# Gated linear attention on one core: the decay of the chunk states applied to the queries, and the steps of two heads interleaved on TensorE

## The chip, the cores and the metric

The kernel runs on one core of a Trainium2 chip. The metric is the device time of one execution in microseconds (us). The engines are named as in the profile: PE (TensorE, with PEld for its weight loads), DVE (VectorE), ACT (ScalarE), POOL (GpSimd), and SP, which issues the DMAs.

## The reference, cut to what matters

The program is one encoder layer on two sequences of 512 tokens: a SwiGLU half step, a mixer of gated linear attention (GLA, 4 heads) beside grouped-query attention, an output projection, a second SwiGLU half step and a gated embedding. The change lies in GLA, in one direction of which the reference computes, by chunks of 64 tokens (`b` is the running sum of the log decay within a chunk):

```
cum = cumsum(log_a)          # within a chunk
mid, last = cum at the chunk's middle, at its end
scores  = (q * exp(cum - mid)) @ (k * exp(mid - cum)).T, masked
o_intra = scores @ v
upd     = (k * exp(last - cum)).T @ v
state_{c+1} = exp(last_c) * state_c + upd_c
o_inter = (q * exp(cum)) @ state_c
o = o_intra + o_inter
```

The forward direction includes the token itself, the backward one doesn't. The sum of both goes through an RMS norm per head and a swish gate.

## The kernel before

The GLA steps are short, and between them TensorE works on the output projection of the other half of the mixer. TensorE's order is written by hand: generators yield after each piece of work, and `main.weave(order(), pieces, end)` puts one piece of GLA after every one or two ticks of `main`, where a tick is three products of 128x512 (L707, called main products below). The other engines' order is made by a scheduler from the order in which the code issues work and from its dependences. Matmul results that aren't main products go to a pool of four PSUM banks (`pd`); a step that needs a bank waits until the earlier user's readers are done.

Two generators `A` and `B` do the two sequences, each with four heads h, in pairs that share `pre`. The steps are:

- `pre(hp)` (L990 to L1008): loads log decay and q, k of two heads, sums the decay with a product (`b`), takes exponentials on ScalarE (`E`), and makes on VectorE the scaled queries and keys `z` (tile `qk1`, named qk in the profile): eight products of 64x512. Rows 0 to 63 hold the forward direction, 64 to 127 the backward one. `R` (128 x 8) holds for each chunk the decay between the middles of neighbouring chunks.
- `one(h)` has three pieces. kT: TensorE transposes the keys (L1022), ScalarE copies them. U: eight products of keys and values give the chunks' updates in two banks (L1029); ScalarE starts the states W with the first and the last chunk (L1036, L1037), and VectorE runs the recurrence over the chunks, six updates in each direction, alternating (L1039, L1041); then GpSimd multiplies all states by R (L1042, L1043). S: eight products give the scores of both directions (L1051), and VectorE copies them under the masks into A (L1053).
- `two_a(h)`: TensorE adds A times v (L1062) and scaled queries times W (L1065) in one bank; ScalarE squares it (osq, L1068), VectorE sums (oss, L1070), makes the norm's factor and multiplies four blocks with the gate into Gh (L1073).
- `two_b(h)`: TensorE transposes Gh (L1080), ScalarE and VectorE write it into mixG (L1081, L1082), which the output projection reads later.

States are kept relative to a chunk's middle, hence the factor R between the recurrence's state and the one that a query of the next chunk uses. The evacuations of the main products on VectorE (L1099, L1101, with statistics at L509) and the splits of weights into two parts (L137 on ScalarE, L138 on GpSimd or VectorE) run beside all this.

In `order()`, a pair of heads runs one(0), one(1), two_a(0), two_a(1), then pre of the next pair, then two_b(0), two_b(1).

Of the kernel before, what the change touches and what calls it, by code (L numbers as in the profile page):

```python
# [13 lines left out]
ALU = mybir.AluOpType  # L14
# [6 lines left out]
NT = 4  # L21
# [9 lines left out]
PLAN = dict(s0=102,  # L31
            s1=112,
            d0=(8, 14, 20, 26, 32),
            sB=(52, 56, 60, 75, 77),
            d1=(90, 96, 102, 108, 117),
            A=(157, 159, 160),
            seg=((2, 132), (2, 142), (18, 160), (18, 170), (43, 193), (43, 216), (178, 334)),
            b=(4, 3),
            end=415)
# [675 lines left out]
class Middle:  # L715
# [246 lines left out]
    def gla(self, s):  # L962
        nc, L = self.nc, self.L
        f, bw = slice(0, 64), slice(64, 128)
        T = {}

        def pre(hp):
            if hp == 0:
                T["mx"] = L.xp.tile([128, 4, 2, 512], F32R, tag="x", name="mixG")
                self.mix[s, 0] = T["mx"]  # L970
                T["A"] = self.vp.tile([128, 2, NT, 128], F32, tag="v", name="A")
                nc.gpsimd.memset(T["A"], 0.0)
            lq = self.m8("lq", (128, 2, 2, 512))
            l, qk = lq[:, 0].rearrange("p d (t c) -> p d t c", t=NT), lq[:, 1]
            for t in range(NT):
                nc.sync.dma_start(l[:, :, t], self.spill["l", s][t].rearrange("p (d c) -> p d c", d=2)[:, :, hp * 128:(hp + 1) * 128])
            for i in range(2):
                nc.sync.dma_start(qk[:, i], self.spill["gqk", s][2 * i + hp])
            yield
            R = [self.sp.tile([128, 8], F32, tag=f"R{e}", name=f"R{e}", bufs=2) for e in range(2)]  # L980
            E = self.m8("E", (128, 2, 2, 512))
            z = self.m8("qk1", (128, 2, 2, 512))
            for e in range(2):
                T["z", 2 * hp + e], T["R", 2 * hp + e] = z[:, e], R[e]
            for dr in range(2):
                sc = self.sp.tile([128, 2, 8], F32, tag="sc", name="sc")
                for hf in range(2):
                    b = L.bank_d().rearrange("p (a n) -> p a n", a=2)
                    for a in range(2):
                        nc.tensor.matmul(b[:, a, :132], l[:, dr, 2 * hf + a], self.L.U[:, dr], start=True, stop=True)  # L990
                    for j, sg in ((0, 1.0), (1, -1.0)):
                        L.expln(E[:, dr, j, hf * 256:(hf + 1) * 256].rearrange("p (a n) -> p a n", a=2),
                                             b[:, :, :128], AF.Exp, scale=sg)
                    nc.vector.tensor_copy(
                        sc[:, :, hf * 4:hf * 4 + 4].rearrange("p k (a c) -> p a k c", a=2),
                        b[:, :, 128:132].rearrange("p a (k c) -> p a k c", k=2))
                    if hf == 0:
                        yield
                ex = self.sp.tile([128, 7], F32, tag="ex", name="ex")
                if dr == 0:  # L1000
                    nc.vector.tensor_tensor(ex, sc[:, 1, 0:7], sc[:, 0, 1:8], ALU.add)
                else:
                    nc.vector.tensor_tensor(ex, sc[:, 1, 1:8], sc[:, 0, 0:7], ALU.add)
                for e in range(2):
                    rs, rd = slice(64 * e, 64 * e + 64), slice(64 * dr, 64 * dr + 64)
                    L.expln(R[e][rd, 1 - dr:8 - dr], ex[rs], AF.Exp)
                    for i in range(2):
                        nc.vector.tensor_tensor(z[rd, e, i], qk[rs, i], E[rs, dr, i], ALU.mult)  # L1008
                yield

        def one(h):
# [6 lines left out]
            q1, k1 = T["z", h][:, 0], T["z", h][:, 1]  # L1018
            R = T["R", h]
            b = L.bank_d()  # L1020
# [2 lines left out]
            kT = self.m2("kT", shape=(128, NT, 128))  # L1023
            nc.scalar.activation(kT.rearrange("p a n -> p (a n)"), b, AF.Copy)
            yield
            U = [L.bank_d().rearrange("p (c n) -> p c n", c=4) for _ in range(2)]
            for c in range(8):
                rw = slice(64 * (c % 2), 64 * (c % 2) + 64)
# [9 lines left out]
            for c in range(1, 7):  # L1038
                nc.vector.scalar_tensor_tensor(W[f, c + 1], W[f, c], R[f, c:c + 1], up(c, f), ALU.mult, ALU.add)  # L1039
                cb = 7 - c  # L1040
                nc.vector.scalar_tensor_tensor(W[bw, cb - 1], W[bw, cb], R[bw, cb:cb + 1], up(cb, bw), ALU.mult, ALU.add)  # L1041
            nc.gpsimd.tensor_tensor(W[f, 1:8], W[f, 1:8], R[f, 1:8].unsqueeze(2).to_broadcast([64, 7, 128]), ALU.mult)  # L1042
            nc.gpsimd.tensor_tensor(W[bw, 0:7], W[bw, 0:7], R[bw, 0:7].unsqueeze(2).to_broadcast([64, 7, 128]), ALU.mult)  # L1043
            yield
            A = T["A"][:, h % 2]
            S = [L.bank_d().rearrange("p (a n) -> p a n", a=NT) for _ in range(2)]
            for t in range(NT):
                ts = slice(t * 128, (t + 1) * 128)
                for dr in range(2):
                    rd = slice(64 * dr, 64 * dr + 64)  # L1050
                    nc.tensor.matmul(S[dr][:, t], k1[rd, ts], q1[rd, ts], start=True, stop=True)  # L1051
            for dr in range(2):
                nc.vector.copy_predicated(A, self.L.mask[:, dr].unsqueeze(1).to_broadcast([128, NT, 128]), S[dr])  # L1053
            T["h", h] = gv, G, W, A
            yield

# [87 lines left out]
def build(tc, d, outs):  # L1144
    nc = tc.nc
    ctx = ExitStack()
    with ctx:
# [36 lines left out]
        with ExitStack() as mctx:  # L1184
# [50 lines left out]
            def order():  # L1235
                yield from A00
                for _ in range(PLAN["b"][0]):
                    yield
                yield from A[1](0)
                yield from A[1](1)  # L1240
                yield from A[2](0)
                yield from A[2](1)
                yield from A[0](1)
                yield from A[3](0)
                yield from A[3](1)
                yield from A[1](2)
                yield from A[1](3)
                yield from A[2](2)
                yield from A[2](3)
                yield from B[0](0)  # L1250
                yield from A[3](2)
                yield from A[3](3)
                yield from B[1](0)
                yield from B[1](1)
                yield from B[2](0)
                yield from B[2](1)
                yield from B[0](1)
                yield from B[3](0)
                yield from B[3](1)
                yield from B[1](2)  # L1260
                yield from B[1](3)
                yield from B[2](2)
                yield from B[2](3)
                for _ in range(PLAN["b"][1]):
                    yield
                yield from B[3](2)
                yield from B[3](3)
            main.weave(order(), 60 - len(PLAN["A"]) + PLAN["b"][0] + PLAN["b"][1], PLAN["end"])
            main.end()

# [158 lines left out]
```

## Time and profile before

| | us |
|---|---|
| three runs | 1990.23, 1979.57, 1983.87 |
| median | 1983.87 |
| profiled execution, its time | 1983.58 |
| its span | 1981.8 |
| GLA's stage, first kT to last two_b (1031.68 to 1165.77 in the span) | 134.09 |
| busy in that stage: PE / DVE / ACT / POOL | 115.78 / 107.47 / 42.58 / 54.83 |

The times are of the whole program; the span is from the first to the last instruction of the profiled execution. Times in timelines count from the span's start. A row of a timeline has start, duration, engine, line, operation, tile written and read, and, in brackets, how long the engine was idle before it and what ended that. A row of the windows has the stretch, its length, and per engine busy time and instructions, then the mean granted clock of TensorE and the DMA's share and rate. A row of the waits names who waited for whom: total, times, longest. In rows of TensorE on these small tiles the profile counts a product of full precision twice (x16 for eight).

### The profile page before, as it was taken

The numbers are of one execution on the slowest core, as the hardware profiler recorded it, in microseconds if no ns is written. First come the engines' busy times: TensorE is split into PE (matmuls) and PEld (weight loads), VectorE is DVE, ScalarE is ACT, GpSimd is POOL, SyncE is SP. The second block draws the span as 40 slices with busy tenths as digits, with TensorE's granted clock in tenths as the row PEclk, the third lists the DMA queues.
The fourth block names the chain that finished last, engine by engine and source line by source line (L and its number), as shares of the span: only waits on it lengthen the run. The fifth ranks groups of instructions, "written<-read, shape, count | busy, mean of one in ns | idle before, by whom it ended". The sixth has DMA issues, their size and how long they took to land. (4 is left out here: it accounts for less than half of the span.)

```text
span 1981.8 us, 25356 instructions
## 1 busy us (share of the span) xinstructions
PE 1879.1 (95%) x8838; PEld 1534.9 (77%) x8838; DVE 1367.1 (69%) x2068; ACT 883.4 (45%) x1670; POOL 950.2 (48%) x710
## 2 busy tenths in 40 slices
PE   7999999999999797989998888999999999799999
PEld 5788888888788686877876667888888888588787
DVE  7856566574656974778778879566566575855973
ACT  5445444444221444757852337445444444221342
POOL 0665565554761254342234343654665555762253
PEclk9999999999999998999999999999999999899999
DMA  4425444478666233222443331435434478576142
GB/s 177 156 105 177 168 150 152 148 288 337 268 248 211 73 126 111 77 80 91 133 143 101 94 117 66 158 109 185 161 141 170 155 297 338 206 267 255 54 128 85
DMA packets 104959, 322.22 MB, mean 163 GB/s; under 512 B 11008, under 2 KB 38400, under 8 KB 99456
## 3 DMA queue, kind: packets, MB, share of 16 engines
q1 hardware_dynamic: 104832, 320.61, 44.9%
q8 instruction: 70, 1.15, 0.2%
q14 instruction: 57, 0.47, 0.1%
HBM read 218.85 MB, written 101.71 MB: 162 GB/s over the span
## 5 line engine op out<-in xcount | busy, mean ns | idle before, releaser
L138 POOL TENSOR_TENSOR w<-raw,w 128x512 fp32r<-128x512 f32 (+1 forms) x372 | 511.4, 1385 | 773.8 <-ACT w L137 714.7
L137 ACT ACTIVATE w<-raw 128x512 fp32r<-128x512 f32 (+1 forms) x586 | 363.5, 624 | 444.5 <-POOL raw L269 107.8
L425 PE MATMUL pm<-X,w 128*128 128x512 f32 x1848 | 435.0, 393 | 11.0 <-ACT X L137 8.2
L269 POOL TENSOR_TENSOR raw<-raw 128x512 f32<-128x512 f32 x240 | 348.0, 1458 | 155.6 <-DMA raw<-in_wgu 81.7
L425 PEld LDWEIGHTS pm<-X,w 128*128 128x128 f32 x1848 | 347.9, 189 | 89.5 <-ACT X L137 8.8
L425 PE MATMUL pd<-X,w 128*128 128x512 f32 x1320 | 309.2, 392 | 2.9 <-DVE w L138 2.2
L138 DVE TENSOR_TENSOR w<-raw,w 128x512 fp32r<-128x512 f32 x214 | 220.3, 1035 | 126.0 <-ACT w L137 116.4
L425 PEld LDWEIGHTS pd<-X,w 128*128 128x128 f32 x1320 | 248.5, 189 | 58.0 <-DVE w L138 3.0
L536 PE MATMUL pm<-w,XB 128*128 128x512 f32 x864 | 202.5, 394 | 5.5 <-POOL w L138 5.4
L707 PE MATMUL pm<-w,h1T 128*128 128x512 f32 (+1 forms) x768 | 183.9, 382 | 22.6 <-ACT gr L749 11.4
L536 PEld LDWEIGHTS pm<-w,XB 128*128 128x128 f32 x864 | 163.3, 190 | 42.8 <-POOL w L138 9.1
L138 DVE TENSOR_TENSOR hs<-sg,hs 128x512 fp32r<-128x512 f32 (+1 forms) x182 | 143.8, 810 | 49.5 <-ACT hs L137 48.4
L137 ACT ACTIVATE hs<-sg 128x512 fp32r<-128x512 f32 (+1 forms) x182 | 98.4, 561 | 164.8 <-DVE sg L391 64.4
L707 PEld LDWEIGHTS pm<-w,h1T 128*128 128x128 f32 x768 | 135.9, 194 | 45.0 <-ACT gr L749 11.7
L536 PE MATMUL pd<-w,XB 128*128 128x512 f32 x648 | 151.2, 393 | 15.5 <-issue 14.8
L536 PEld LDWEIGHTS pd<-w,XB 128*128 128x128 f32 x648 | 122.8, 190 | 42.0 <-issue 15.2
L523 DVE TENSOR_TENSOR Y<-Y,pm 128x512 f32<-128x512 f32 x104 | 70.6, 684 | 61.5 <-PE pm L536 61.3
L523 DVE TENSOR_TENSOR Y<-Y,pd 128x512 f32<-128x512 f32 x88 | 59.9, 684 | 60.0 <-PE pd L536 57.3
L707 PE MATMUL pm<-w,h3T 128*128 128x512 f32 x384 | 90.8, 393 | 0.9 <-DVE h3T L662 0.9
L371 DVE TENSOR_TENSOR sg<-u,pm 128x512 f32<-128x512 f32 x22 | 15.1, 687 | 109.3 <-PE pm L425 109.3
L707 PEld LDWEIGHTS pm<-w,h3T 128*128 128x128 f32 x384 | 71.2, 188 | 15.8 <-DVE h3T L662 1.4
L652 ACT ACTIVATE pd<-pd,c_lnT 128x512 f32<-128x512 f32 x48 | 36.0, 752 | 100.4 <-PE pd L650 100.4
(237 smaller groups left out, 2554.0 us busy)
## 6 DMA issues: line engine op xcount, KB each, us to landing
hs<-hs SPq DMA_DIRECT2D x126, 512.0 KB, 2.6
XB<-hs SPq DMA_DIRECT2D x42, 1536.0 KB, 6.8
raw<-in_wgu SPq DMA_DIRECT2D x88, 512.0 KB, 3.5
raw<-in_wd SPq DMA_DIRECT2D x36, 512.0 KB, 6.4
hs_t<-hs SPq DMA_DIRECT2D x56, 256.0 KB, 2.5
XB<-hs_t SPq DMA_DIRECT2D x26, 512.0 KB, 5.2
raw<-in_wout SPq DMA_DIRECT2D x16, 512.0 KB, 3.6
raw<-in_wpg SPq DMA_DIRECT2D x16, 512.0 KB, 3.5
```

The lines of the kernel that those rows point to most:

```text
L137: first = nc.scalar.activation(hi, raw, AF.Copy)
L138: (eng or nc.vector).tensor_tensor(lo, raw, hi.bitcast(F32), ALU.subtract)
L269: (sums or self.nc.gpsimd).tensor_tensor(o(), x(), y(), ALU.subtract)
L371: add = lambda o, x, y: nc.vector.tensor_tensor(o, x, y, ALU.add)
L425: nc.tensor.matmul(bank, w[:, a, kt * 128:(kt + 1) * 128], X[k][:, kt, b], start=(k in (0, 1, 4) and kt == 0 and m == 0), stop=(kt == 3 an ...
L523: nc.vector.tensor_tensor(yv, yv, bank, ALU.add)
L536: nc.tensor.matmul(b[t], h[:, a, t * 128:(t + 1) * 128], d[:, c], start=(k in (0, 4, 1) and g == 0 and x == 0), stop=(g == len(H) - 1 and ...
L652: nc.scalar.activation(p, p, AF.Identity, scale=self.lnT[:, c:c + 1], bias=self.lnT[:, c + 8:c + 9])
L707: nc.tensor.matmul(banks[t][:, :width], x[:, i, t * 128:(t + 1) * 128], w[a][:, j], start=(q == 0 and a == 0 and m == 0), stop=(q == nq - ...
```

## The change

Two things are done. First, the states are no longer multiplied by R on GpSimd. Instead, after the scores have been computed from the scaled queries q1, VectorE multiplies q1 in place by R, chunk by chunk (128x512, R spread over 64 columns), and two_a uses these queries. For that the scores come ahead of the states in `one(h)`, and R is zeroed first (a memset of 128x8 per head on GpSimd), since the chunk without a predecessor now has a factor too. Second, `order()` no longer runs both heads of a pair through one step and then the next: the second head's kT and S come before the first head's two_a, its U comes between the first head's two_a and two_b, and its own two_b comes after the next pair's pre.

```diff
             for e in range(2):
+                nc.gpsimd.memset(R[e], 0.0)
                 T["z", 2 * hp + e], T["R", 2 * hp + e] = z[:, e], R[e]
...
             nc.scalar.activation(kT.rearrange("p a n -> p (a n)"), b, AF.Copy)
             yield
+            A = T["A"][:, h % 2]
+            S = [L.bank_d().rearrange("p (a n) -> p a n", a=NT) for _ in range(2)]
+            for t in range(NT):
+                ts = slice(t * 128, (t + 1) * 128)
+                for dr in range(2):
+                    rd = slice(64 * dr, 64 * dr + 64)
+                    nc.tensor.matmul(S[dr][:, t], k1[rd, ts], q1[rd, ts], start=True, stop=True)
+            for dr in range(2):
+                nc.vector.copy_predicated(A, self.L.mask[:, dr].unsqueeze(1).to_broadcast([128, NT, 128]), S[dr])
+            qc = q1.rearrange("p (c n) -> p c n", c=8)
+            nc.vector.tensor_tensor(qc, qc, R.unsqueeze(2).to_broadcast([128, 8, 64]), ALU.mult)
+            yield
             U = [L.bank_d().rearrange("p (c n) -> p c n", c=4) for _ in range(2)]
...
-            nc.gpsimd.tensor_tensor(W[f, 1:8], W[f, 1:8], R[f, 1:8].unsqueeze(2).to_broadcast([64, 7, 128]), ALU.mult)
-            nc.gpsimd.tensor_tensor(W[bw, 0:7], W[bw, 0:7], R[bw, 0:7].unsqueeze(2).to_broadcast([64, 7, 128]), ALU.mult)
-            yield
...
             T["h", h] = gv, G, W, A
             yield
...
+                def two(H, p, nxt):
+                    g = [H[1](p), H[1](p + 1)]
+                    for j in (0, 0, 0, 1, 1):
+                        next(g[j])
+                        yield
+                    yield from H[2](p)
+                    next(g[1])
+                    yield
+                    yield from H[3](p)
+                    yield from H[2](p + 1)
+                    yield from nxt
+                    for _ in range(PLAN["b"][1] if nxt is last else 0):
+                        yield
+                    yield from H[3](p + 1)
+                last = ()
+                yield from two(A, 0, A[0](1))
+                yield from two(A, 2, B[0](0))
+                yield from two(B, 0, B[0](1))
+                yield from two(B, 2, last)
```

(`H[0]` to `H[3]` are pre, one, two_a and two_b; the removed lines of `order()` called them in the order told above.) Of before and after, what follows is the program's own order on an engine; qk_8660 is the tile of the first pair's queries and keys, gvh the values.

TensorE before, from U of the first head to two_a of the first head:

```order
L1029 MATMUL pd<-gvh,kT 128x128 x8
L707 MATMUL pm<-w,mixA 128x512 x6
L1051 MATMUL pd<-qk_8660 128x128 x8
L707 MATMUL pm<-w,mixA 128x512 x3
L1022 MATMUL pd<-c_ident,qk_8660 128x128 x4
L707 MATMUL pm<-w,mixA 128x512 x3
L1029 MATMUL pd<-gvh,kT 128x128 x8
L707 MATMUL pm<-w,mixA 128x512 x3
L1051 MATMUL pd<-qk_8660 128x128 x8
L707 MATMUL pm<-w,mixA 128x512 x6
L1062 MATMUL pd<-gvh,A 128x128
L1065 MATMUL pd<-W,qk_8660 64x128 x2
```

Here both heads' U and S are done before the first two_a. TensorE after, between the same two steps of the first head:

```order
L1042 MATMUL pd<-gvh,kT 128x128 x8
L707 MATMUL pm<-w,mixA 128x512 x3
L1023 MATMUL pd<-c_ident,qk_8660 128x128 x4
L707 MATMUL pm<-w,mixA 128x512 x3
L1033 MATMUL pd<-qk_8660 128x128 x8
L707 MATMUL pm<-w,mixA 128x512 x3
L1063 MATMUL pd<-gvh,A 128x128
L1066 MATMUL pd<-W,qk_8660 64x128 x2
```

The first head's S now stands ahead of these rows, and the second head's U behind them. TensorE after, from the end of the first head's two_a to the start of the second's:

```order
L707 MATMUL pm<-w,mixA 128x512 x6
L1042 MATMUL pd<-gvh,kT 128x128 x8
L707 MATMUL pm<-w,mixA 128x512 x3
L1081 MATMUL pd<-c_ident,Gh 128x128 x4
L707 MATMUL pm<-w,mixA 128x512 x3
L1063 MATMUL pd<-gvh,A 128x128
L1066 MATMUL pd<-W,qk_8660 64x128 x2
```

Before, only three main products stood between the two two_a; now U of the second head and two_b of the first do too. VectorE before, from the end of the second head's recurrence to the first head's Gh:

```order
L1041 SCALAR_TENSOR_TENSOR W<-W,R_8658,pd 64x128
L1053 COPY_PREDICATED A<-c_mask,pd 128x512
L1099 SCALAR_TENSOR_TENSOR h_8498<-h_8498,pm 128x512
L1053 COPY_PREDICATED A<-c_mask,pd 128x512
L1070 TENSOR_REDUCE oss<-osq 128x4
L1099 SCALAR_TENSOR_TENSOR h_8500<-h_8500,pm 128x512
L782 TENSOR_SCALAR gnv<-oss 128x4
L186 SCALAR_TENSOR_TENSOR gna<-gnv,gny 128x4
L187 TENSOR_TENSOR gna<-gna,gny 128x4
L188 SCALAR_TENSOR_TENSOR gny<-gna,gny 128x4
L1073 SCALAR_TENSOR_TENSOR Gh<-pd,gny,Gh 128x128 x4
```

The second head's recurrence is done ahead of the first head's norm. VectorE after, from the second head's masked scores to the start of its recurrence:

```order
L1035 COPY_PREDICATED A<-c_mask,pd 128x512
L1037 TENSOR_TENSOR qk_8660<-qk_8660,R_8658 128x512
L1035 COPY_PREDICATED A<-c_mask,pd 128x512
L1071 TENSOR_REDUCE oss<-osq 128x4
L1100 SCALAR_TENSOR_TENSOR h_8498<-h_8498,pm 128x512
L782 TENSOR_SCALAR gnv<-oss 128x4
L186 SCALAR_TENSOR_TENSOR gna<-gnv,gny 128x4
L187 TENSOR_TENSOR gna<-gna,gny 128x4
L188 SCALAR_TENSOR_TENSOR gny<-gna,gny 128x4
L1074 SCALAR_TENSOR_TENSOR Gh<-pd,gny,Gh 128x128 x4
L1052 SCALAR_TENSOR_TENSOR W<-W,R_8658,pd 64x128
L1054 SCALAR_TENSOR_TENSOR W<-W,R_8658,pd 64x128
```

The first head's norm and Gh (down to L1074) now stand ahead of the second head's recurrence (L1052, L1054, twelve rows in turn), so the second head's W comes after the first head's G.

More of the change, by code (lines that the diff above doesn't have):

```diff
@@ L1041, in one @@
                 nc.vector.scalar_tensor_tensor(W[bw, cb - 1], W[bw, cb], R[bw, cb:cb + 1], up(cb, bw), ALU.mult, ALU.add)
-            nc.gpsimd.tensor_tensor(W[f, 1:8], W[f, 1:8], R[f, 1:8].unsqueeze(2).to_broadcast([64, 7, 128]), ALU.mult)
-            nc.gpsimd.tensor_tensor(W[bw, 0:7], W[bw, 0:7], R[bw, 0:7].unsqueeze(2).to_broadcast([64, 7, 128]), ALU.mult)
-            yield
[L1045 to L1053, printed above, removed]
             T["h", h] = gv, G, W, A
@@ L1238, in order @@
                     yield
[L1239 to L1264, printed above, removed]
-                    yield
-                yield from B[3](2)
-                yield from B[3](3)
+                def two(H, p, nxt):
[5 more added lines that the diff above has]
+                    next(g[1])
+                    yield
+                    yield from H[3](p)
[9 more added lines that the diff above has]
+                yield from two(B, 2, last)
             main.weave(order(), 60 - len(PLAN["A"]) + PLAN["b"][0] + PLAN["b"][1], PLAN["end"])
```

## The prediction

> **What bounds the kernel now.** I read the page, then the stage that the change touches in the view of windows, then TensorE's waits in it, then the timelines of TensorE, VectorE and GpSimd.
>
> ```profile
> span 1981.8 us, 25356 instructions
> PE 1879.1 (95%) x8838; PEld 1534.9 (77%) x8838; DVE 1367.1 (69%) x2068; ACT 883.4 (45%) x1670; POOL 950.2 (48%) x710
> ...
> core 0: us, PE busy (x) PEld busy (x) DVE busy (x) ACT busy (x) POOL busy (x), PEclk, DMA share, GB/s
> 1031.68:1165.77 134.09, 115.78 (x773) 84.67 (x773) 107.47 (x258) 42.58 (x109) 54.83 (x50) 0.96 0.32 97
> ...
> PE pd L1022 <- DVE W L1039: 7.5, 4, 3.1
> PE pd L1022 <- DVE qk L1008: 5.5, 4, 1.8
> PE pd L1062 <- DVE W L1039: 5.3, 4, 1.3
> PE pd L1080 <- DVE Gh L1073: 0.7, 1, 0.7
> ```
>
> TensorE bounds the kernel. The stage from the first kT to the last two_b is 134.09 us long; TensorE is busy 115.78 of it and VectorE 107.47. All that TensorE waits for there is VectorE: 7.5 + 5.5 + 5.3 + 0.7 = 19.0 us. GpSimd releases nothing for TensorE. So the change can win at most some 19 us and the clock that these waits cost (below), 1.2% of the time. It moves no work off TensorE: its products and transposes are those of before in another order. What counts is how much TensorE has to do between the start of a VectorE chain and the step that needs its end. I call that the cover.
>
> ```profile
> 1031.68 0.63 PE L1022 MATMUL pd<-c_ident,qk 128*128 128x128 f32 x4 [1.02 <-DVE qk L1008]
> 1032.07 0.95 PE L707 MATMUL pm<-w,mixA 128*128 128x512 f32 x3
> 1033.00 1.16 PE L1029 MATMUL pd<-gvh,kT 64*128 64x128 f32 x16
> 1034.09 1.66 PE L707 MATMUL pm<-w,mixA 128*128 128x512 f32 x6
> 1035.68 1.16 PE L1051 MATMUL pd<-qk 64*128 64x128 f32 x16
> 1036.78 0.96 PE L707 MATMUL pm<-w,mixA 128*128 128x512 f32 x3
> 1039.07 0.63 PE L1022 MATMUL pd<-c_ident,qk 128*128 128x128 f32 x4 [1.33 <-DVE W L1039]
> ...
> 1046.46 0.46 PE L1062 MATMUL pd<-gvh,A 128*128 128x128 f32 x2 [1.33 <-DVE W L1039]
> ...
> 1049.58 0.97 PE L707 MATMUL pm<-w,mixA 128*128 128x512 f32 x3
> ...
> 1060.88 0.60 PE L1080 MATMUL pd<-c_ident,Gh 128*128 128x128 f32 x4
> 1061.24 0.95 PE L707 MATMUL pm<-w,mixA 128*128 128x512 f32 x3
> 1062.02 0.60 PE L1080 MATMUL pd<-c_ident,Gh 128*128 128x128 f32 x4
> ```
>
> These are the steps of the first pair of heads (start, duration, idle before it). From start to start: kT 0.39 us, three main products 0.93 behind kT and 0.78 elsewhere, six 1.59, states U 1.09, scores S 1.10, two_a 3.12 (1046.46 to 1049.58), two_b 0.36. The reader is to see the two waits of 1.33: both end with the recurrence W on VectorE, which holds the PSUM banks of U.
>
> ```profile
> 1034.79 0.34 DVE L1039 SCALAR_TENSOR_TENSOR W<-W,R,pd 64x128 f32<-64x128 f32 x1 [1.21 <-ACT W L1037]
> ...
> 1038.96 0.35 DVE L1041 SCALAR_TENSOR_TENSOR W<-W,R,pd 64x128 f32<-64x128 f32 x1
> 1039.34 1.58 DVE L1053 COPY_PREDICATED A<-c_mask,pd 128x512 f32<-128x512 uint32 x2
> ...
> 1050.39 0.69 DVE L1070 TENSOR_REDUCE oss<-osq 128x4 f32<-128x512 f32 x1 [1.72 <-ACT osq L1068]
> 1050.99 0.68 DVE L1099 SCALAR_TENSOR_TENSOR h<-h,pm 128x512 f32<-128x512 f32 x1
> ...
> 1052.85 1.13 DVE L1073 SCALAR_TENSOR_TENSOR Gh<-pd,gny,Gh 128x128 f32<-128x128 f32 x4
> ...
> 1081.68 0.46 PE L1062 MATMUL pd<-gvh,A 128*128 128x128 f32 x2 [1.33 <-DVE W L1039]
> ...
> 1087.72 1.13 DVE L1073 SCALAR_TENSOR_TENSOR Gh<-pd,gny,Gh 128x128 f32<-128x128 f32 x4
> ```
>
> Two chains follow. W: from the start of U (1033.00) to the step that its end lets go (1039.07) 6.07 us, of it 4.5 for the twelve updates (1034.79 to 1039.31). G: from the start of two_a to the end of the four Gh products 7.52 us in the first pair (1046.46 to 1053.98), 0.60 of it an evacuation (L1099) of the main products, and 7.17 in the second (1081.68 to 1088.85).
>
> **The change part by part.** *The multiply.* Sixteen GpSimd products go, eight VectorE products of 128x512 with two SBUF inputs and eight memsets of R come.
>
> ```profile
> L1042 POOL TENSOR_TENSOR W<-W,R x8: 1676/1677/1680, 1039.0 to 1153.2; 64x896 f32<-64x896 f32 x8
> L1043 POOL TENSOR_TENSOR W<-W,R x8: 1679/1682/1684, 1040.8 to 1154.9; 64x896 f32<-64x896 f32 x8
> ...
> L1008 DVE TENSOR_TENSOR qk<-lq,E x32: 673/685/1785, 1025.2 to 1135.6; 64x512 f32<-64x512 f32 x32
> ...
> 1032.92 0.20 POOL L1033 MEMSET W<- 64x128 f32 x1 [2.85 <-DVE qk L1008]
> ```
>
> GpSimd loses 8 x (1.677 + 1.682) = 26.9 us. It releases nothing that TensorE waits for (the waits above), so this is worth 0; at most, if VectorE's waits hid it, the two products in a row would stand on the path once a pair, 4 x 3.36 = 13.4. The new multiply isn't in the trace; nearest is L1008, half as many partitions, the same 512 columns: 0.69, and 1.79 at worst. I take 0.69 (0.60 from start to start). It stands between the two masked copies of the scores (0.72 each, 1.9 us for the three). For the first head these lie under six main products and the wait for U: 1.59 + 1.79 (1033.00 to 1034.79) against 1.9, 1.5 us to spare. For the second head they lie under two_a, whose square reaches VectorE 3.93 us after its start (1046.46 to 1050.39), with one evacuation 2.5 us, 1.4 to spare. So it costs 0; without the cover it would be 8 x 0.69 = 5.5. The memsets take 0.20 at most; in the last two pairs they wait for the W chain that read the old R, and in GpSimd's queue splits of weights (L138) stand behind them, which also wait for ScalarE's half of the split: 0; at worst a split comes late by a W chain, 4.5 us in each of two pairs. SP's queue keeps its order but for six loads of gv, G and l that move by a few places; nothing in this stage of TensorE waits for them, and with S ahead of U gv is needed later than before: 0.
>
> *The order on TensorE.* The wait is chain less cover, less 0.18: 1033.00 to 1039.07 is 6.07, the cover there 1.09 + 1.59 + 1.10 + 0.78 = 4.56, and the profile shows 1.33 instead of 1.51, since it counts idle time from the modelled end of a pipelined matmul.
>
> Term 1, first head's W. It now holds up two_a of the same head. Cover: U 1.09, main 0.78, kT 0.39, main 0.93, S 1.10, main 0.78 = 5.07. Wait 0.82 in place of 1.33. In the later pairs evacuations came in front of the chain (7.5 for the four, not 5.3); now TensorE runs S ahead of U and leaves room for them, except in the last pair, where two evacuations and two statistics stand there, 0.4 us late. Four pairs: 3.7 (3.3 if none is late; 5.5 if the old 2.2 us of lateness stays), against 7.5.
>
> Term 2, second head's W. Before, its cover was short by 1.33, 5.3 in all. Now VectorE's program has G of the first head in front of it (in the second pair one update is ahead): two_a of the second head needs G and then W. Chain from the start of two_a(first): 7.17 + 4.5 + 0.15 to reach TensorE = 11.8, and 12.4 in the two pairs where an evacuation stands in it. Cover: two_a 3.12, six main 1.5, U 1.09, main 0.78, two_b 0.36, main 0.78, the first product with A 0.39 = 8.0. Wait 3.6 or 4.2 per pair, split between two_b (for the first Gh) and two_a (for W): 15.6 in all (14.4 with no evacuation in it, 16.8 with one in each).
>
> Term 3, qk to the next pair's kT. Both orders run G of the second head and then the eight L1008. Between two_a(second) and kT there were 30 main products and two two_b; now there are 27 and one, 0.78 + 0.36 = 1.1 less cover. The first wait (1.0) stays, the three others grow: 5.5 + 3.3 = 8.8. This chain is long because of collisions:
>
> ```profile
> 1063.10 4.11 DVE L1008 TENSOR_TENSOR qk<-lq,E 64x512 f32<-64x512 f32 x3
> ...
> 1062.98 1.27 POOL L138 TENSOR_TENSOR w<-raw,w 128x512 fp32r<-128x512 f32 x1 [5.20 <-ACT w L137]
> 1064.83 1.82 POOL L138 TENSOR_TENSOR w<-raw,w 128x512 fp32r<-128x512 f32 x1 [0.58 <-ACT w L137]
> ```
>
> Three L1008 took 4.11 us beside two splits on GpSimd, 1.37 each against 0.69. The splits follow the main products, and pre comes one step earlier among them, so I keep the collisions. If they fall elsewhere, the three waits lose up to 2.3 us each: 3.6 in all. If the last pair's statistics also stand in it, 10.
>
> Term 4, the last two_b. It lay behind 15 main products, another two_b and three more and waited 0.7; now behind 15 alone, 1.2 less: 1.9 (0.7 if G comes faster without the other head's).
>
> Sum of waits: 3.7 + 15.6 + 8.8 + 1.9 = 30.0 against 19.0, +11.0; ends 22.0 (+3.0) and 34.2 (+15.2).
>
> *The clock.* Rows of the stage cut at the 3.41 us steps in which the granted clock changes:
>
> ```profile
> 1113.70:1117.12 3.42, 2.14 (x18) 1.00 0.49 153
> 1117.12:1120.53 3.41, 3.41 (x15) 0.50 0.07 19
> ...
> 1151.25:1154.66 3.41, 2.07 (x15) 1.00 0.02 5
> 1154.66:1158.08 3.42, 3.42 (x27) 1.00 0.00 0
> ```
>
> A step with 3.42 - 2.14 = 1.28 us idle was followed by half the clock, one with 1.34 wasn't. Each throttled step costs 1.7 us (half of 3.41). The stage's mean clock of 0.96 is 0.04 x 134.09 = 5.4 us lost, three such steps. Term 2 puts 3 to 4 us of waiting close together in each pair, so about four steps there: +1.7 (none more: 0; with most other waits, seven: +6.8).
>
> The Trainium skill ("TensorE: Matmul & The Clock Gate", HAM oscillation) gives as the rule that gaps under about 3.4 us don't throttle. By it no wait here would, and the sum would be 1.7 us less. The rows above disagree: 1.28 us idle was enough once.
>
> The profiled execution took 1983.58 us (span 1981.8), 0.3 under the median of the three runs shown, 1983.87. 1983.6 + 11.0 + 1.7 = 1996.3; I say 1996, 0.6% more. Faster or slower by 0.5% (9.9 us) is about what a measurement of this kernel tells from no change, and the forecast lies just beyond it.
>
> **The rivals.** *VectorE catches up: no change.* If the L1008 escape the splits and no evacuation falls into G, the waits are 22.0, the clock as now: 1986.6; with one throttled step less 1985. For it: VectorE isn't full (107.47 of 134.09), and GpSimd has 26.9 us less to collide with. Against it: the collisions seen are with L138, which stays, and the W updates took 0.34 to 0.36 beside L1042 and L1043 as elsewhere. It decides where term 3 falls under 5. Chance 0.29.
>
> *GpSimd was the hidden limit: faster.* If the interleaving hid both W chains and nothing waited for the decay, 7.5 + 5.3 us of waits and three throttled steps (5.1) would go: 1965.7. It needs W of the second head to run before two_a comes, so ahead of G or with G done 4 us sooner; VectorE's order has G in front in three pairs of four. Chance 0.06.
>
> The Trainium skill ("GPSIMD Engine Reference", Engine selection) sends an elementwise multiply to VectorE, about twice as fast with two inputs, and so speaks for the change. The prices agree (3.36 us against 0.69), but in this trace none of it is waited for.
>
> *The waits feed on each other: 2001 to 2008.* Waits at their upper ends (+15.2) and seven throttled steps (+6.8) give 2005.6. For it: the throttled step at 1117.12 follows the wait in front of a two_a, and a two_a at half the clock starts the next G later. Against it: a chain on VectorE that waits for TensorE gains the same time to catch up. It decides where more than five steps are throttled. Chance 0.12.
>
> **How the numbers follow.** The forecast has 0.53, its own range is 1990 to 2001; about a fifth of it lies under 1993.8. Slower: 0.53 x 0.8 + 0.12 = 0.55; faster 0.06; same 0.39. The range 1984 to 2004 leaves out the fast rival, the lowest part of the first and the upper part of the last, 0.15 to 0.2.
>
> **What would show it.** In the profile after: two_b's first transpose and the first product with W of each second head wait for Gh and W on VectorE, together 3 to 4.5 us per pair (term 2; under 2 refutes it); two_a of each first head waits under 1.2 (term 1); kT of the next pair waits 2 to 3 for qk (term 3; under 1 is the first rival). The new multiply is at 0.69 and ends no wait of TensorE. The stage is some 11 to 13 us longer, the rest as long as before. I would be wrong if VectorE's G chain ran well under 7 us, or if the stage of the wout products behind it, which I leave as it is, gave time back.

## The result, and the profile after

The changed kernel took 2010.62 us (median of 4 runs, 2009.04 to 2011.46). The kernel before, run in turn with it, took 1987.05 us (4 runs, 1979.57 to 1991.74). The ratio is 1.0133 with a 95% interval of 1.0107 to 1.0159: slower by 1.3%, against a forecast of 0.6%, and above the stated range of 1984 to 2004. The medians differ by 23.6 us. The profiled execution took 2010.11 us, 26.5 more than the profiled one of before; the accounts below are of these two.

First the page of after, the span and the busy time of each engine:

```profile
span 2008.3 us, 25351 instructions
PE 1898.3 (95%) x8838; PEld 1547.5 (77%) x8838; DVE 1373.3 (68%) x2076; ACT 883.1 (44%) x1670; POOL 922.8 (46%) x702
```

TensorE has as many instructions as before (x8838) and is busy 19.2 us longer. Then the stage from the first kT to the last two_b, in the view of windows of after:

```profile
core 0: us, PE busy (x) PEld busy (x) DVE busy (x) ACT busy (x) POOL busy (x), PEclk, DMA share, GB/s
1030.73:1190.45 159.72, 133.62 (x772) 96.13 (x773) 113.51 (x267) 42.50 (x109) 27.06 (x38) 0.83 0.28 86
```

The stage grew from 134.09 to 159.72 us, by 25.6 of the 26.5, so nearly all of the difference lies in it. Idle time is the stage less the busy time: 18.3 us before, 26.1 after, 7.8 more. The other 17.8 us are TensorE being *busy* longer with the same products (115.78 to 133.62, x773 and x772). The column PEclk tells why: a mean granted clock of 0.83 in place of 0.96. Cut at the 3.41 us steps of the clock, the stage has 16 steps at half clock, where it had three.

TensorE's waits after, in the view of waits for the window around the stage:

```profile
PE pd L1066 <- DVE W L1054: 11.9, 4, 3.3
PE pd L1023 <- DVE qk L1009: 9.4, 4, 4.3
PE pd L1081 <- DVE Gh L1074: 3.0, 3, 1.7
PE pd L1063 <- DVE W L1052: 2.7, 4, 0.8
```

Together 27.0 us against 19.0. TensorE's timeline of after shows the largest kind of wait, in the first pair, and what stands behind it:

```profile
1049.19 0.38 PE L1063 MATMUL pd<-gvh,A 128*128 128x128 f32 x2
1052.85 0.70 PE L1066 MATMUL pd<-W,qk 128*64 128x128 f32 x4 [3.28 <-DVE W L1054]
1053.48 0.80 PE L1063 MATMUL pd<-gvh,A 128*128 128x128 f32 x2
...
1056.91 0.70 PE L1066 MATMUL pd<-W,qk 128*64 128x128 f32 x4
1057.54 4.19 PE L707 MATMUL pm<-w,mixA 128*128 128x512 f32 x9
```

The second head's two_a starts, waits 3.28 us for W behind its first product, and then runs at half clock: 0.70 and 0.80 us where the first head's like products took 0.44 and 0.49 at full clock, and nine main products take 4.19 us. The windows of after, cut at the clock's steps, first with all of TensorE's work and then with the main products (L707) alone:

```profile
1047.92:1051.33 3.41, 1.65 (x9) 1.10 (x8) 3.15 (x11) 1.32 (x2) 1.19 (x1) 1.00 0.16 46
1051.33:1054.75 3.42, 1.90 (x10) 1.12 (x10) 2.63 (x6) 0.00 (x0) 0.19 (x2) 0.50 0.00 0
1054.75:1058.16 3.41, 3.41 (x16) 2.13 (x15) 0.00 (x0) 0.48 (x1) 0.00 (x0) 0.50 0.00 0
1058.16:1061.57 3.41, 3.41 (x10) 2.67 (x9) 2.45 (x6) 1.16 (x4) 1.27 (x1) 0.50 0.00 0
1061.57:1064.99 3.42, 3.42 (x22) 3.04 (x21) 2.34 (x10) 1.80 (x6) 0.00 (x0) 1.00 0.74 222
```

```profile
1054.75:1058.16 3.41, 0.62 (x2) 0.50 0.00 0
1058.16:1061.57 3.41, 3.41 (x9) 0.50 0.00 0
```

One wait of 3.28 us is followed by three steps at half clock. The middle one is the one to look at: TensorE is busy all of it (3.41 of 3.41), with two_a's small products and 0.62 us of main products, and the next step is at half clock again. Of these three, only the step that main products filled (3.41) is followed by the full clock. The 16 steps fall like this: 13 behind the waits of the second heads' two_a and two_b (3, 4, 3 and 3 in the four pairs), three behind waits at kT (one behind 2.47 us, two behind 4.33 us).

### The profile page after: what moved, and what is told of

Read it like the earlier page. It is cut to its first block, busy times and chain, and to the rows that moved or that the text cites. A ratio compares the mean times of both kernels' runs of the same rounds, so it can differ in the third digit from the quotient of the medians.

```text
span 2008.3 us, 25351 instructions
## 1 busy us (share of the span) xinstructions
PE 1898.3 (95%) x8838; PEld 1547.5 (77%) x8838; DVE 1373.3 (68%) x2076; ACT 883.1 (44%) x1670; POOL 922.8 (46%) x702
## 4 chain that ended last, share of the span: by engine, by line
PE 44%; DVE 8%; POOL 2%; issue 2%; ACT 1%; DMA 1%; DVEq 0%; SPq 0%; ACTq 0%; POOLq 0%
PE pm L425 12%; PE pd L425 9%; PE pm L707 7%; PE pm L536 5%; PE pd L536 2%; PE pm L772 2%; PE pd L915 1%; PE pd L931 1%; PE pd L901 1%; PE pd L1066 1%; DVE W L1052 1%; DVE W L1054 1%; PE pd L1063 1%; DVE qk L1009 1%; POOL raw L269 1%
## 5 line engine op out<-in xcount | busy, mean ns | idle before, releaser
L707 PE MATMUL pm<-w,h1T 128*128 128x512 f32 (+1 forms) x768 | 183.8, 382 | 22.5 <-ACT gr L749 11.3
L707 PEld LDWEIGHTS pm<-w,h1T 128*128 128x128 f32 x768 | 135.9, 194 | 44.9 <-ACT gr L749 11.6
L707 PE MATMUL pm<-w,h3T 128*128 128x512 f32 x384 | 90.8, 393 | 0.9 <-DVE h3T L662 0.9
L707 PEld LDWEIGHTS pm<-w,h3T 128*128 128x128 f32 x384 | 71.3, 188 | 15.9 <-DVE h3T L662 1.4
```

The source lines that it names most:

```text
L707: nc.tensor.matmul(banks[t][:, :width], x[:, i, t * 128:(t + 1) * 128], w[a][:, j], start=(q == 0 and a == 0 and m == 0), stop=(q == nq - ...
```

## Experiments

Two theories stood against each other. Theory A: a wait costs its own length and, through the clock, half of the work in the half-clock steps that follow, and small products behind the wait keep the clock at half. Theory C: the waits alone make the time, and the clock only goes with them. An expectation that names another theory says what that is. In this table "idle" is the stage less TensorE's busy time, and "busy" grows with the half-clock steps, since all kernels issue the same products in the stage (x772 or x773):

| kernel | time, us | ratio to before, 95% | stage | busy | idle | half-clock steps |
|---|---|---|---|---|---|---|
| before | 1983.3 to 1987.8 | 1 | 134.09 | 115.78 | 18.3 | 3 |
| after | 2010.62 | 1.0107 to 1.0159 | 159.72 | 133.62 | 26.1 | 16 |
| order only | 2043.9 | 1.0271 to 1.0321 | 191.43 | 141.23 | 50.2 | 25 |
| decay only | 1976.65 | 0.9941 to 0.9975 | 126.00 | 114.89 | 11.1 | 2 |
| scores ahead only | 1994.78 | 1.0027 to 1.0070 | 141.34 | 124.31 | 17.0 | 8 |
| after, two_a split | 2004.89 | 1.0076 to 1.0123 | 155.12 | 126.00 | 29.1 | 11 |
| after, short recurrence | 1976.55 | 0.9930 to 0.9964 | 128.41 | 113.70 | 14.7 | 2 |
| wait in two_a | 2000.12 | 1.0054 to 1.0103 | 152.85 | 127.45 | 25.4 | 12 |
| wait at kT | 1999.81 | 1.0057 to 1.0105 | 145.22 | 120.28 | 24.9 | 9 |
| wait at kT, 2nd | 2002.43 | 1.0048 to 1.0118 | 148.37 | 121.08 | 27.3 | 10 |
| wait in two_a, split | 1998.73 | 1.0050 to 1.0110 | 151.73 | 122.23 | 29.5 | 7 |
| one piece more | 1978.92 | 0.9953 to 0.9986 | 127.54 | 116.81 | 10.7 | 3 |

Two thirds of the extra time between before and after is in the column busy. Less half of the time that TensorE was busy in half-clock steps, this column is 107 to 112 us in every row, so it is the clock that moves it. The first row's times are the medians of before in the different comparisons.

**The two halves of the change apart.** The order alone, with the decay on GpSimd as before:

```diff
             for dr in range(2):
                 nc.vector.copy_predicated(A, self.L.mask[:, dr]...)
-            qc = q1.rearrange("p (c n) -> p c n", c=8)
-            nc.vector.tensor_tensor(qc, qc, R..., ALU.mult)
             yield
...
+            nc.gpsimd.tensor_tensor(W[f, 1:8], W[f, 1:8], R[f, 1:8]..., ALU.mult)
+            nc.gpsimd.tensor_tensor(W[bw, 0:7], W[bw, 0:7], R[bw, 0:7]..., ALU.mult)
```

> The interleaved order of the changed kernel, with the decay as before (two GpSimd products on the states; no multiply of the queries, no memset of R). Theory A (the order makes a long wait inside the second head's two_a, and the clock lost behind it is most of the 26 us): at least as slow as the changed kernel, since GpSimd's 3.36 us now lie on the way to two_a: waits of some 6 us there, 2020 to 2040 us, 14 or more half-clock steps of 3.41 us in the stage. Theory B (the eight multiplies on VectorE and the scores ahead of the states cost the time, the order little): about as before, 1980 to 1992 us.

It took 2043.9 us, 57 more than before and above the 2020 to 2040 that Theory A gave. Its waits, and its stage:

```profile
PE pd L1065 <- POOL W L1053: 36.9, 8, 6.4
PE pd L1022 <- DVE qk L1008: 9.5, 4, 4.3
```

```profile
1031.41:1222.84 191.43, 141.23 (x773) 100.69 (x773) 109.62 (x259) 42.41 (x109) 53.37 (x50) 0.78 0.23 71
```

GpSimd now releases every two_a, 36.9 us in all. The order of before had other work between the recurrence and two_a, and the interleaved order hasn't.

The decay alone (queries scaled, scores ahead), with the order of before:

```diff
             def order():
...
-                yield from two(A, 0, A[0](1))
...
+                yield from A[1](0)
+                yield from A[1](1)
+                yield from A[2](0)
+                yield from A[2](1)
+                yield from A[0](1)
+                yield from A[3](0)
+                yield from A[3](1)
...
```

> The decay on the queries, with the scores ahead of the states, in the old order of the two heads (both through one, then both two_a). Theory A: no wait stands in front of the second two_a, the first one has both W chains behind it with more cover than before; waits 10 to 19 us in the stage, at most 4 half-clock steps, 1972 to 1986 us. Theory B: 2000 to 2012 us.

It took 1976.65 us (12 runs), 0.4% less than before: faster than both kernels. The waits and the stage:

```profile
PE pd L1023 <- DVE qk L1009: 5.4, 4, 2.1
PE pd L1042 <- DVE W L1052: 4.5, 4, 2.0
PE pd L1066 <- DVE W L1054: 1.3, 3, 0.8
```

```profile
1031.13:1157.13 126.00, 114.89 (x773) 86.16 (x773) 110.97 (x266) 42.08 (x109) 28.10 (x38) 0.97 0.35 104
```

So the loss comes from the order, which costs 34 us on top of the decay. The two halves don't simply add: in the interleaved order the decay's move is worth 33 us (2043.9 to 2010.62). With the order of before, the wait of two_a for W fell from 5.3 to 1.3, that for the states' banks from 7.5 to 4.5, and one half-clock step went.

To part the multiply from the scores' place, the scores were taken ahead while GpSimd still multiplied W, in the order of before (the decay-only kernel with the first of the two diffs above, L1053 as there).

> The kernel before in its order and with its decay on GpSimd, the scores alone taken ahead of the states. Theory A: GpSimd's multiplication of W still stands between the recurrence and two_a, but the main products that stood between the scores and two_a no longer cover it for the second head: waits at two_a of the second head 1 to 4 us a pair, stage 136 to 150 us, time 1985 to 2000. Rival: the gain of the run with the decay on the queries comes from the scores' place alone: then 1975 to 1981 here.

It took 1994.78 us, so the scores' place alone loses, and in two_a it is now GpSimd that TensorE waits for:

```profile
PE pd L1065 <- POOL W L1053: 9.5, 7, 3.0
```

```profile
1030.25:1171.59 141.34, 124.31 (x772) 92.24 (x773) 109.31 (x255) 42.37 (x109) 54.30 (x50) 0.90 0.30 90
```

This run speaks most directly against Theory C: TensorE is idle 1.3 us less than before (17.0 against 18.3), and yet the kernel is slower by 0.3 to 0.7%. All of the loss is busy time, 8.5 us, with eight half-clock steps in place of three. Six of the eight lie behind waits of 2.7 to 3.0 us inside the second head's two_a.

With the scores ahead, the multiply's move to the queries is worth 18 us (1994.78 to 1976.65). In the kernel before it hid behind the scores.

**The wait taken away.** The changed kernel, with the recurrence left out for both heads: one operation of 64x768 for each direction stands in place of its six updates, so the states are not those of the reference.

```diff
-            for c in range(1, 7):
-                nc.vector.scalar_tensor_tensor(W[f, c + 1], W[f, c], R[f, c:c + 1], up(c, f), ALU.mult, ALU.add)
-                cb = 7 - c
-                nc.vector.scalar_tensor_tensor(W[bw, cb - 1], W[bw, cb], R[bw, cb:cb + 1], up(cb, bw), ALU.mult, ALU.add)
+            wide = lambda x: x.to_broadcast([64, 6, 128])
+            nc.vector.scalar_tensor_tensor(W[f, 2:8], wide(W[f, 1:2]), R[f, 1:2], wide(U[1][f, 0:1]), ALU.mult, ALU.add)
+            nc.vector.scalar_tensor_tensor(W[bw, 0:6], wide(W[bw, 6:7]), R[bw, 6:7], wide(U[0][bw, 3:4]), ALU.mult, ALU.add)
```

> The changed kernel with the recurrence of the states left out: one VectorE instruction of 64x768 per direction in place of six updates of 64x128, some 1.8 us in place of 4.5, so the output is another one. Theory A: the waits for W in two_a fall from 11.9 us to under 3, those in front of the first two_a (2.7) go, the half-clock steps behind them go with them (4 to 6 left, behind the waits for qk); 1976 to 1988 us. Theory C the same. If the clock is lost for another reason (small products in a row, wherever they wait), 12 or more steps stay and it is 1992 us or more.

```profile
1031.94:1160.35 128.41, 113.70 (x772) 83.80 (x773) 96.57 (x187) 42.40 (x109) 27.25 (x38) 0.97 0.35 103
```

The time is 1976.55 us. Against after, idle time fell by 11.4 us and busy time by 19.9, both on TensorE, whose products were not touched; of the 16 half-clock steps two are left, fewer than the four to six expected. The second heads' waits for W fell from 11.9 to 3.2 us, a little more than expected, and the first heads' 2.7 us are gone. So the recurrences set both: the waits, and the clock behind them. Since both heads' recurrences are shorter here, the run doesn't part the two, but of the waits for W in after, only the second heads' had half-clock steps behind them.

**The same waits, other work behind them.** In the changed kernel, six main products were moved from behind the second head's two_a to behind its first block, which is where W is waited for:

```diff
                     nc.tensor.matmul(o[64 * cc:64 * cc + 64, t], q1[...], W[:, c], start=False, stop=True)
+                if h % 2 and t == 0:
+                    yield
...
-                    yield from H[2](p + 1)
+                    rest = H[2](p + 1)
+                    next(rest)
+                    main.to(main.n + 2)
+                    yield from rest
```

> The changed kernel, but six of the main products that follow the second head's two_a are moved into it, behind its first block, so that the wait for W is followed by main products and not by small ones. Theory A (a wait loses several half-clock steps because two_a's small products behind it don't bring the clock back): the wait for W stays at 3 to 3.5 us, two half-clock steps less behind each, 8 to 11 in the stage instead of 16; G of the second head comes 1.4 us later at full clock, so the waits for qk grow by some 1 us each; 1996 to 2007 us. Theory C (the length of a wait alone sets how long the clock stays low): 15 to 17 steps, and with the later G 2010 to 2016 us.

```profile
PE pd L1023 <- DVE qk L1009: 12.1, 4, 4.2
PE pd L1066 <- DVE W L1054: 11.9, 4, 3.3
```

```profile
1033.81:1188.93 155.12, 126.00 (x773) 91.15 (x773) 112.50 (x268) 42.39 (x109) 27.30 (x38) 0.88 0.27 84
```

The wait for W is the same 11.9 us, idle time is 3.0 us more, and yet the kernel is 5.7 us faster, since the half-clock steps fell from 16 to 11 and busy time by 7.6. Behind the second heads' two_a and two_b they fell from 13 to 7; behind the longer waits at kT (3.38 to 4.20 us in three pairs) they rose from three to four. By Theory C it would have been 3 us slower.

**Waits put in on purpose.** To see the clock's part without the interleaving, the decay-only kernel got multiplications by 1.0 in place. First four of the second head's W, ahead of its two_a:

```diff
+            if h % 2:
+                w = W.rearrange("p c n -> p (c n)")
+                for _ in range(4):
+                    nc.vector.tensor_scalar(w, w, 1.0, None, op0=ALU.mult)
             T["h", h] = gv, G, W, A
```

> The decay on the queries and the scores ahead, in the order of before (stage 126.7 us, waits 12.2 us, two half-clock steps), plus four multiplications of the second head's W by 1.0 after its recurrence, some 1 to 1.3 us each (an estimate from the 128x1024 op on VectorE), so that the second head's two_a waits about 4 us longer, with nothing but small products of the pair behind it. Theory A (the clock steps lose the time, and a wait costs more of them where small products follow it): waits 24 to 30 us, 10 to 14 half-clock steps, stage 150 to 165 us. Theory C (only the waits cost, wherever they lie): stage 126.7 plus the added waits, 138 to 145 us, and the same number of steps as in the run with the same multiplications put ahead of kT.

Then three of the first head's queries and keys, ahead of kT, where main products stand between the small ones:

```diff
                         nc.vector.tensor_tensor(z[rd, e, i], qk[rs, i], E[rs, dr, i], ALU.mult)
+                if dr == 1:
+                    w = z[:, 0].rearrange("p i n -> p (i n)")
+                    for _ in range(3):
+                        nc.vector.tensor_scalar(w, w, 1.0, None, op0=ALU.mult)
                 yield
```

> The same base, plus three multiplications by 1.0 of the next pair's queries and keys at the end of pre, so that kT waits about 4 us; between kT and the next small products stand main products. Theory A: waits 22 to 28 us, 5 to 9 half-clock steps, one or two for each wait, stage 142 to 152 us: fewer steps for each us of waiting than with the wait in two_a. Theory C: as many steps as there; the stages differ by the waits alone.

The stages, of the wait in two_a and of the wait at kT:

```profile
1029.26:1182.11 152.85, 127.45 (x773) 94.27 (x774) 119.41 (x281) 42.08 (x109) 28.34 (x38) 0.87 0.28 85
```

```profile
1033.58:1178.80 145.22, 120.28 (x772) 90.41 (x773) 114.81 (x272) 42.21 (x109) 29.17 (x34) 0.90 0.29 85
```

Over the decay-only kernel, the wait in two_a added 14.3 us of idle and 12.6 of busy time; its stage lies in Theory A's range (150 to 165) and above Theory C's (138 to 145). The wait at kT added 13.8 us of idle, another 4.05 in front of the first kT and so ahead of the stage, and 5.4 of busy time. Per microsecond of waiting the clock cost 0.9 us in two_a and 0.3 at kT. The totals came out alike (2000.12 and 1999.81) because the waits at kT were longer than planned: 5.07 to 7.14 us each, against 3.77 to 4.80 in two_a. So a second try put four multiplications straight behind the first head's own products, meant to make the waits at kT equal to those in two_a.

> As the run with the wait at kT, but with four multiplications (0.69 us each) straight behind the first head's own queries and keys, so that kT waits 3.2 to 5 us, as long as the second head's two_a in the run with the wait there (3.8 to 4.8 us; 26.4 us of idle, 12 half-clock steps, 17.9 us lost in them). Theory A (what follows the wait decides how many steps it costs): idle 24 to 28 us, 6 to 9 half-clock steps, 8 to 13 us lost in them, stage 4 to 10 us shorter than there, 1990 to 1997. Rival (the length of the wait alone decides): 11 to 13 steps, 16 to 20 us lost, 1998 to 2003.

```profile
1038.26:1186.63 148.37, 121.08 (x772) 91.02 (x773) 116.92 (x275) 42.23 (x109) 29.17 (x34) 0.89 0.27 83
```

As a match it failed: VectorE ran the second head's products among the multiplications, the waits were 5.90 to 7.86 us, and the time, 2002.43, lies in the rival's range and not in Theory A's. The 10 steps lie between the two. But it speaks against the rival that length alone decides: four waits of 28.4 us in all cost 10 steps and 6.2 us of busy time, while 17.6 us of waits in two_a cost 11 of the 12 steps and most of the 12.6 us there. What isn't parted by this pair is how much of it comes from the longer waits holding whole steps of idle time, in which half a clock costs nothing.

The better test keeps the place of the wait, comes close to its length (3.27 to 5.71 us against 3.77 to 4.80), and changes what follows. The kernel with the wait in two_a, with six main products behind the first block of the second head's two_a:

```diff
                     nc.tensor.matmul(o[64 * cc:64 * cc + 64, t], q1[...], W[:, c], start=False, stop=True)
+                if h % 2 and t == 0:
+                    yield
+                    yield
...
-            yield
+            if h % 2 == 0:
+                yield
...
-            main.weave(order(), 60 - len(PLAN["A"]) + ..., PLAN["end"])
+            main.weave(order(), 64 - len(PLAN["A"]) + ..., PLAN["end"])
```

> As the run with the wait in two_a (2000.12 us; 26.4 us of idle, 12 half-clock steps, 17.9 us lost in them), with the same four multiplications of the second head's W, but with six main products between the first block of its two_a, at which the wait lies, and the other three blocks. Theory A (small products behind a wait hold the clock at half): 6 to 9 half-clock steps, 9 to 14 us lost in them, 1991 to 1998. Rival (the length of the wait alone decides): 11 to 13 steps, 16 to 20 us lost, 1998 to 2004.

The clock's steps behind the first such wait, without the main products (windows of the kernel with the wait in two_a) and with them:

```profile
1046.51:1049.92 3.41, 0.00 (x0) 0.00 (x0) 3.40 (x7) 0.41 (x2) 0.11 (x1) 1.00 0.06 18
1049.92:1053.33 3.41, 2.18 (x11) 1.33 (x12) 2.45 (x9) 0.00 (x0) 0.00 (x0) 0.50 0.21 59
1053.33:1056.75 3.42, 3.42 (x14) 2.22 (x15) 0.14 (x1) 0.60 (x1) 0.00 (x0) 0.50 0.00 0
1056.75:1060.16 3.41, 3.41 (x11) 2.86 (x11) 1.40 (x3) 1.83 (x6) 1.87 (x2) 0.50 0.00 0
1060.16:1063.57 3.41, 3.41 (x20) 2.92 (x20) 3.22 (x12) 1.53 (x6) 0.69 (x1) 1.00 0.43 137
```

```profile
1047.36:1050.78 3.42, 0.00 (x0) 0.00 (x0) 3.42 (x9) 0.41 (x2) 0.00 (x0) 1.00 0.14 42
1050.78:1054.19 3.41, 3.29 (x10) 2.48 (x11) 2.02 (x7) 0.00 (x0) 0.00 (x0) 0.50 0.05 16
1054.19:1057.60 3.41, 3.41 (x24) 2.32 (x23) 0.34 (x1) 1.28 (x3) 1.26 (x1) 1.00 0.00 0
...
1030.28:1182.01 151.73, 122.23 (x773) 90.20 (x773) 119.39 (x282) 42.14 (x109) 27.38 (x38) 0.92 0.29 88
```

Both waits (4.78 and 4.91 us) filled a whole step (0.00 busy). With small products behind it three half-clock steps follow, with six main products one. Over the four pairs, 3, 3, 2 and 3 steps follow this wait without the main products, and 1, 3, 1 and 1 with them; the second pair, with the longest wait (5.71), didn't gain. Over the stage 12 steps became seven and busy time fell by 5.2 us, as Theory A expected. The time did not follow (1998.73 against 2000.12, intervals that overlap; Theory A's range ended at 1998), because idle time rose by 4.1 us: kT waits 3.1 us more, the last two_b 1.9 and two_a 1.1, and U 1.9 less.

**A kernel that beats both?** The decay-only kernel does. One more piece of main products between the two two_b of a pair was tried on top, in all four pairs (told here in the lines of the decay-only kernel; the run writes the same order as a list of steps):

```diff
-                yield from A[3](0)
-                yield from A[3](1)
+                yield from A[3](0)
+                yield
+                yield from A[3](1)
...
-            main.weave(order(), 60 - len(PLAN["A"]) + ..., PLAN["end"])
+            main.weave(order(), 64 - len(PLAN["A"]) + ..., PLAN["end"])
```

> The decay on the queries and the scores ahead, in the order of before, and one more piece of main products between the two two_b of a pair. Theory A: the wait for W at the second two_a or at kT loses up to 1 us a pair, no new half-clock step: 1972 to 1979, against 1976.65 without it. Rival: the piece is missed where the next pair's waits stand, and qk waits longer: 1978 to 1984.

It took 1978.92 us (12 runs), no better than without (the intervals overlap); idle time fell by 0.4 us and one more half-clock step came.

## Why the prediction was wrong

The direction was right and so was the mechanism of the waits. The step that failed is the clock: "about four steps there: +1.7", with seven as its upper end. There were 16. Thirteen more steps of 1.7 us are 22 us; about 4 us of that fell on idle time, and 17.8 us of busy time came of it, ten times the term. The same error sits in the rival of the waits that feed on each other: its mark of "more than five steps" was passed, but its price rested on seven.

- The error in the reasoning was to price a wait by one step. The rows of before show single steps, and each of those held three main products, as the windows of before for L707 alone show:

```profile
1072.74:1076.15 3.41, 1.63 (x3) 0.50 0.74 231
1117.12:1120.53 3.41, 1.65 (x3) 0.50 0.07 19
1144.42:1147.83 3.41, 1.63 (x3) 0.50 0.00 0
```

The change puts the wait *inside* two_a, with three quarters of its small products directly behind it and main products only after those. The forecast counted how long waits are and how many, and not what TensorE runs in the steps behind them. With two_a split, and with the wait put in on purpose, the runs show that this counts beside the length.
- Term 1 (first head's W): 3.7 predicted, 2.7 measured. As expected, under 1.2 for each.
- Term 2 (second head's G, then W): 15.6 predicted. W took 11.9 and Gh 3.0, of which the last two_b's 1.19 is term 4: 13.7. Per pair 3.4 against 3 to 4.5 expected.
- Term 3 (qk to the next kT): 8.8 predicted, 9.4 measured. The waits were 1.01, 1.63, 2.47 and 4.33 us, so they spread more than the 2 to 3 foreseen. The total is near by luck: against before the four grew by 0, 0, 1.4 and 2.5 us, where 0 and three times 1.1 were reckoned.
- Term 4 (the last two_b): 1.9 predicted, 1.2 measured. The sum of waits was 27.0 where 30.0 was predicted, +8.0 in place of +11.0.
- The multiply: eight of 0.675 us on VectorE, and no engine waited for it, as predicted (0.69). The 3.36 us that the prediction set beside it are two products with 3.5 times as many columns; per column GpSimd was 1.4 times as slow (1.68 us for 896, 0.675 for 512). That GpSimd's product was worth nothing held for the kernel before only. Taken by itself, the decay on the queries with the scores ahead gains 0.4%, a part that the sum had at zero: in the old order the waits for W fell from 12.8 to 5.8 us.
- The rest of the program stayed as it was: 0.9 us of the 26.5 lie outside the stage.
- The first rival (VectorE catches up) decided at a term 3 under 5; it was 9.4. GpSimd as the hidden limit showed up where it wasn't looked for, in the interleaved order without the moved decay: 36.9 us of waits. There the decay's move, which the sum had at zero, is worth 33 us.

The Trainium skill ("TensorE: Matmul & The Clock Gate", HAM oscillation) has gaps over about 3.4 us as the ones that throttle. The waits of 3.27 and 3.28 us in two_a are under that and were followed by three half-clock steps each, and in before a wait of 1.84 us at kT was followed by one (1072.74), so the trace disagrees. The same page (Part 1, The HAM clock gate) says that about 3.4 us of sustained busy time bring back the full clock. The trace agrees for the step that main products filled (1058.16), and not for the busy step before it (1054.75), which had 0.62 us of them.

## What to carry to other kernels

Price a wait of TensorE as its length and half of the work in the half-clock steps behind it, and read from the order what stands behind it: here a step full of wide products brought the clock back, and a run of small ones kept it at half for up to three. When a chain on another engine can't be covered, try to let the wait fall in front of wide products, not in the middle of a group of small ones, and look what the moved products leave open: it was worth 5.7 us in one kernel, and in another the waits elsewhere took the gain back. And test the halves of a change apart: here one gains 0.4%, and the other, put on top of it, loses 34 us.

## What was unexpected of the hardware

That a step in which TensorE was busy throughout could be followed by another at half clock. In before and after, what sets such steps apart is how much of the main products they hold. These are half-clock steps of after, again with L707 alone; the first, second, fourth and fifth were followed by another half-clock step, the third and sixth by the full clock:

```profile
1092.29:1095.70 3.41, 0.00 (x0) 0.50 0.08 24
1095.70:1099.12 3.42, 1.26 (x3) 0.50 0.00 0
1099.12:1102.53 3.41, 2.95 (x7) 0.50 0.00 0
...
1181.04:1184.46 3.42, 0.87 (x2) 0.50 0.00 0
...
1153.73:1157.14 3.41, 1.63 (x3) 0.50 0.00 0
1157.14:1160.55 3.41, 1.85 (x4) 0.50 0.00 0
```

In before and after, steps with up to 1.26 us of main products were followed by half the clock, steps with 1.85 or more by the full one. With 1.63 to 1.65 both came: the full clock in before, half in after at 1088.88 and 1153.73, where a wait lies in the step too.

The amount of main products alone is not the rule, though. These two steps, of the kernel with two_a split and of the one with the scores ahead alone, hold the same 1.22 us of main products, and TensorE is busy throughout both. The first was followed by the full clock, the second by half:

```profile
1098.87:1102.29 3.42, 1.22 (x3) 0.50 0.00 0
```

```profile
1088.33:1091.75 3.42, 1.22 (x3) 0.50 0.14 41
```

In the first the main products stand at the start of the step, in the second at its end, so the clock seems to follow a stretch that ends somewhat before the step does. An estimate, fitted afterwards to the 108 half-clock steps in the table: take each step 0.4 us earlier and count the time of all other products at 0.4 of that of main products. Then a sum of 2.0 us parts the steps before the full clock from those before half a clock, all but one. In the steps as they stand, main products alone put 17 of the 108 on the wrong side, and all products counted alike 22. No run tested this fit. What it is about the small products (their width, their partitions, or the share of the array that they use) was not tried either.
